# Gate one-hot blocks of a mixture kernel: stationary operand packed per token, moving operand with two tokens innermost

## The chip, the cores and the metric

The kernel runs on one core of a Trainium2 chip. The metric is the device time of one execution in microseconds (us), the median of the runs. The engines are named as the profile names them: PE is the matrix engine (PEld its weight loads, shown apart), DVE the vector engine, ACT the scalar engine, POOL GpSimd, SP the queue that issues most loads.

## The reference

Two models one after the other, two layers each, on 256 tokens of width 1024 (in the first model 256 context tokens run beside them in layer 0). The part that matters here is the feed-forward of the first model, in which 8 heads choose 16 of 16,384 experts for each token; each expert is addressed by two keys of 128:

```
s1, i1 = lax.top_k(s[:, :, 0], 16)
s2, i2 = lax.top_k(s[:, :, 1], 16)
cidx = i1[..., :, None] * 128 + i2[..., None, :]
top_s, pos = lax.top_k(s1[..., :, None] + s2[..., None, :], 16)
eidx = take_along_axis(cidx, pos)
gate = softmax(top_s)
hid = gelu(einsum('td,thkd->thk', x, u_emb[eidx]))
out = einsum('thk,thkd->td', gate * hid, v_emb[eidx])
```

So every token has 128 (head, choice) pairs, each with a first key, a second key and a gate.

## The kernel before

The kernel does not gather the chosen experts. It computes all 16,384 hidden values of every token (128 tiles of 128 experts, the loop over `i` in `peer`), and multiplies them by a gate matrix that is zero where an expert was not chosen. All large products are made from a high and a low part of both factors, three matmuls each (`mm3`, lines 408 to 410), on weights that the DVE, the ACT and at times POOL split into `wh` and `wl` (lines 179 and 190). Layer 0 has T = 512 tokens, so its matmuls have 512 columns; layer 1 has 256.

The gate matrix is made token by token. For one token, with the 128 (head, choice) pairs on the partitions, `Am` holds the one-hot of the second key (128 pairs by 128 keys) and `Bm` the one-hot of the first key times the gate; the product of the two over the pairs is the token's 128 by 128 gate matrix. The gate is kept in two float16 parts, so `Bm` has two halves (n = 0, 1), and a token takes two matmuls of 128 columns that add up in PSUM. `IT` holds the keys and `GT` the gates, in float16, pairs on partitions and tokens along the row.

The one-hots are made for eight tokens at a time (the loop over `q`, lines 1355 to 1369): the DVE compares a table `iota` with the keys (line 1359 for `Am`, line 1360 for `Bk`), and multiplies `Bk` by the two gate parts (line 1365, twice). All tiles have the shape [2, 128, 4]: four tokens lie innermost, so that in every operand the innermost run is four neighbouring float16. A token's operand on the PE is therefore a column of elements that are 8 bytes apart:

```
nc.tensor.matmul(b[:, j * 128:(j + 1) * 128], Am[:, :, j], Bm[:, n, :, j], ...)
```

`flush` (line 1335) takes four tokens: eight such matmuls (line 1343) into one PSUM bank, which the ACT then copies out (line 1344). There are 128 flushes in layer 0 and 64 in layer 1. A flush comes two loop steps after its tiles were made (`pend`); `Am` and `Bm` have three buffers, `Bk` two.

All of this is a side task. The main loop runs the expert tiles, and after every three main matmuls `tick` adds their estimated PE time to a clock; whenever the clock passes the next due time, the side task runs to its next `yield`. So the order of the instructions on each engine is fixed when the program is built, and the side task's place in it depends on estimates, not on measured times. While the gates are made, `W.pool_every` is 0 (line 1328), so all low parts `wl` of the streamed weights are made on the DVE, two tiles ahead of the PE. In layer 0 the DVE also makes modulation sums on the side (line 460).

Of the kernel before, what the change touches and what calls it, by code (L numbers as in the profile page):

```python
# [12 lines left out]
F16 = mybir.dt.float16  # L13
# [3 lines left out]
OP = mybir.AluOpType  # L17
# [330 lines left out]
def tile_dit_peer_conformer(ctx: ExitStack, tc: tile.TileContext, A, out):  # L348
    nc = tc.nc
# [6 lines left out]
    def bankA():  # L356
        return psum.tile([128, 512], F32, name="pA", bufs=4)
# [3 lines left out]
    def bankB():  # L361
        ring[0] += 1
        return psum.tile([128, 512], F32, name="pB", bufs=4)
# [228 lines left out]
    def tproj(key, X, T, bank=None, mid=None):  # L592
        h, lo = W.next(*key)
        p = bankA() if bank is None else bank
        for d in range(8):
            if mid is not None and d == 4:
                mid()
            mm3(p[:, :T], (h[:, d * 128:(d + 1) * 128], lo[:, d * 128:(d + 1) * 128]),
                (X[0][:, d, :T], X[1][:, d, :T]), d == 0, d == 7)
            tick(3 * T / 2.4)  # L600
        return p
# [595 lines left out]
    def peer(l, hcp, kp, keys, early):  # L1197
# [11 lines left out]
        with ExitStack() as st:  # L1209
            pp = st.enter_context(tc.tile_pool(name=f"peer{l}", bufs=1))  # L1210
            IT = pp.tile([128, 2, T], F16, name="IT")
            GT = pp.tile([128, 2, T], F16, name="GT")
            GN = pp.tile([128, nt, 128], F32, name="GN")
            IN = pp.tile([128, nt, 2, 128], F32, name="IN")
            iota = pp.tile([128, 128, 4], F16, name="iota")
            nc.gpsimd.iota(iota, pattern=[[1, 128], [0, 4]], base=0, channel_multiplier=0, allow_small_or_imprecise_dtypes=True)
            gp = st.enter_context(tc.tile_pool(name=f"gel{l}", bufs=3))
            if l == 0:
                ms_stack = ExitStack()
# [34 lines left out]
            def select():  # L1254
                yield from topk_keys()
                yield from route()
# [5 lines left out]
            for c in range(16):  # L1262
                p = early.pop(0)[0] if early else tproj(("wq", l, c), X, T)
                q = tk.tile([128, T], F32, name="q", bufs=4)
# [3 lines left out]
            def route():  # L1268
# [47 lines left out]
                for i in range(3):  # L1316
                    b = bankB()
# [13 lines left out]
                tg = tk_stack.enter_context(tc.tile_pool(name=f"gm{l}", bufs=1))  # L1331
                pend = []
                sg = None

                def flush(q, Am, Bm):
                    nonlocal sg
                    tb, r = divmod(q, TB // 4)
                    if r == 0:
                        sg = tg.tile([128, 128, TB], F32, name="gst", bufs=2)
                    b = bankB()  # L1340
                    for j in range(4):
                        for n in range(2):
                            nc.tensor.matmul(b[:, j * 128:(j + 1) * 128], Am[:, :, j], Bm[:, n, :, j], start=n == 0, stop=n == 1)  # L1343
                    nc.scalar.activation(sg[:, :, r * 4:r * 4 + 4].rearrange("p i t -> p t i"),  # L1344
                                         b.rearrange("p (t i) -> p t i", t=4), AF.Copy, scale=1.0 / GSCALE)
                    if r == TB // 4 - 1:
                        nc.scalar.dma_start(g_d[tb], sg)

                shape = [128, 2, 128, 4]
                iotas = iota[:, None].to_broadcast(shape)  # L1350

                def spread(x, q):
                    return x[:, q * 4:q * 4 + 8].rearrange("p (q t) -> p q t", t=4)[:, :, None, :].to_broadcast(shape)

                for q in range(0, T // 4, 2):
                    Am = tg.tile(shape, F16, name="Am", bufs=3)
                    Bk = tg.tile(shape, F16, name="Bk", bufs=2)
                    Bm = tg.tile([128, 2] + shape[1:], F16, name="Bm", bufs=3)
                    nc.vector.tensor_tensor(Am, iotas, spread(IT[:, 1], q), op=OP.is_equal)
                    nc.vector.tensor_tensor(Bk, iotas, spread(IT[:, 0], q), op=OP.is_equal)  # L1360
                    if len(pend) > 2:
                        flush(*pend.pop(0))
                    yield
                    for n in range(2):
                        nc.vector.tensor_mul(Bm[:, n], Bk, spread(GT[:, n], q))
                    if len(pend) > 2:
                        flush(*pend.pop(0))
                    pend.extend((q + j, Am[:, j], Bm[:, :, j]) for j in range(2))
                    yield
                for x in pend:  # L1370
                    flush(*x)
                    yield
# [31 lines left out]
            b = None  # L1404
            GB = 2 if not last else 4
            for i in range(128):
# [7 lines left out]
                if half == 0:  # L1414
                    b = bankA()
# [4 lines left out]
                if half == 512 // T - 1:  # L1420
                    n = 512 // T
                    j = i % GB - (n - 1)
# [25 lines left out]
            if not last:  # L1448
                for i in range(2):
                    t = hcp.tile([128, D], F32, name=f"hc{i}")  # L1450
# [552 lines left out]
    with tc.tile_pool(name="hcp", bufs=1) as hcp:  # L2003
        norm_ctx = peer(0, hcp, kp, *first)
        kp = ExitStack()
        first = mixer(1, kp, norm_ctx)
    peer(1, None, kp, *first)
    with tc.tile_pool(name="b2", bufs=1) as b2p:
        dec = b2p.tile([128, RET_H, 256], F32, name="dec")
# [154 lines left out]
```

## Time and profile before

| what | value |
|---|---|
| median of 3 runs | 4792.56 us (4787.25 to 4793.66) |
| the profiled execution's own time | 4791.03 us |
| its span, first to last instruction | 4789.2 us |
| mean granted PE clock, share of full speed | 0.984 |
| PE busy | 4624.7 us (97%) |
| DVE busy | 3018.0 us (63%) |
| the gate's 1536 matmuls of line 1343, busy | 213.9 us |
| the gate's 384 DVE operations, busy | 123.8 + 65.9 + 65.8 us |

The spans of one execution are compared with that execution's own time. Busy time of the PE says that some matmul was in flight: matmuls overlap, so what one costs is read from the distance between starts, not from its duration. The time that an engine waits matters only where the engine is the one that sets the pace.

### The profile page before, as it was taken

To read this page: it belongs to the slowest core of one execution; us is meant where nothing else is said; L and a number is where in the kernel's file an instruction comes from. 1 tells how busy PE (TensorE), PEld (TensorE's weight loads), DVE (VectorE), ACT (ScalarE), POOL (GpSimd) and SP (SyncE) were. 2 spreads that over 40 slices of the span, in tenths; PEclk is the share of its full clock that TensorE was granted. 3 is DMA by queue.
4 is the path that set the end of the run, shared out by engine and by line. 5 is a ranking of instruction groups with operands and counts; after the bars stand their busy time and mean duration, and the time that the engine had idled before them with its cause. 6 is when DMAs were issued, how large, how long until landed. Compare 5 with 4: busy or idle time off the path is not lost. (4 is left out here: it accounts for less than half of the span.)

```text
span 4789.2 us, 67997 instructions
## 1 busy us (share of the span) xinstructions
PE 4624.7 (97%) x26438; PEld 3984.8 (83%) x26438; DVE 3018.0 (63%) x4777; ACT 2047.0 (43%) x2979; POOL 1201.8 (25%) x884
## 2 busy tenths in 40 slices
PE   8999999999999999999999999999999988999799
PEld 5787878888888888888798889999888977999788
DVE  6847768798676333333466887765666586555865
ACT  4324443224554322222343454565444444444344
POOL 2412433330000422222213545102442043000510
PEclk9999999999999999999999999999999999999899
DMA  5422222455656655555453346668876533555344
GB/s 218 158 87 64 73 99 95 162 189 198 220 212 226 210 190 190 183 191 191 138 174 106 102 135 226 222 241 293 282 275 221 186 120 119 185 176 171 116 142 158
DMA packets 283357, 831.39 MB, mean 174 GB/s; under 512 B 23688, under 2 KB 106264, under 8 KB 273560
## 3 DMA queue, kind: packets, MB, share of 16 engines
q1 hardware_dynamic: 260960, 715.74, 45.2%
q10 hardware_dynamic: 21896, 110.24, 6.1%
q8 instruction: 207, 3.39, 0.3%
q14 instruction: 118, 0.97, 0.1%
q0 software_dynamic: 176, 1.06, 0.1%
HBM read 724.17 MB, written 102.77 MB: 173 GB/s over the span
## 5 line engine op out<-in xcount | busy, mean ns | idle before, releaser
L190 DVE TENSOR_TENSOR wl<-raw,wh 128x1024 fp32r<-128x1024 f32 (+1 forms) x893 | 1154.1, 1302 | 976.7 <-PE pB L1460 343.1
L179 ACT ACTIVATE wh<-raw 128x1024 fp32r<-128x1024 f32 (+1 forms) x1098 | 1144.1, 1045 | 1072.8 <-issue 709.4
L408 PE MATMUL pA<-xH,wh 128*128 128x256 f32 (+1 forms) x4696 | 1533.8, 327 | 3.6 <-ACT xH L413 1.3
L410 PE MATMUL pA<-xH,wl 128*128 128x256 f32 (+1 forms) x4696 | 1508.3, 321 | 14.1 <-DVE wl L190 12.4
L409 PE MATMUL pA<-xL,wh 128*128 128x256 f32 (+1 forms) x4696 | 1509.8, 322 | 0.5 <-DVE xL L414 0.3
L410 PEld LDWEIGHTS pA<-xH,wl 128*128 128x128 f32 x4696 | 893.3, 190 | 88.6 <-DVE wl L190 16.6
L408 PEld LDWEIGHTS pA<-xH,wh 128*128 128x128 f32 x4696 | 893.9, 190 | 77.9 <-issue 6.0
L409 PEld LDWEIGHTS pA<-xL,wh 128*128 128x128 f32 x4696 | 891.8, 190 | 68.2 <-DVE xL L414 1.1
L190 POOL TENSOR_TENSOR wl<-raw,wh 128x1024 fp32r<-128x1024 f32 (+2 forms) x205 | 479.6, 2342 | 901.2 <-PE pA L410 547.5
L1393 POOL TENSOR_TENSOR gelc<-gelc,gmc 128x512 f32<-128x512 f32 (+1 forms) x256 | 340.0, 1361 | 1004.3 <-DMA gmc<-gmat 699.7
L1460 PE MATMUL pA<-wl,Wh 128*128 128x512 f32 x1024 | 322.4, 395 | 0.0
L1460 PE MATMUL pA<-wh,Wh 128*128 128x512 f32 x1024 | 322.3, 395 | 0.0
L1460 PE MATMUL pA<-wh,Wl 128*128 128x512 f32 x1024 | 322.3, 395 | 0.0
L1344 ACT ACTIVATE gst<-pB 128x512 f32<-128x512 f32 x192 | 216.2, 1126 | 230.5 <-PE pB L1343 229.5
L408 PE MATMUL pA<-wh,xH 128*128 128x256 f32 (+2 forms) x800 | 287.1, 359 | 9.3 <-DVE cu L1833 7.7
L409 PE MATMUL pA<-wl,xH 128*128 128x256 f32 (+2 forms) x800 | 277.6, 347 | 6.5 <-POOL wl L190 5.9
L410 PE MATMUL pA<-wh,xL 128*128 128x256 f32 (+2 forms) x800 | 277.3, 347 | 1.2 <-DVE xL L414 1.1
L414 DVE TENSOR_TENSOR Wl<-gelc,Wh 128x512 fp32r<-128x512 f32 (+1 forms) x256 | 160.6, 628 | 171.3 <-ACT Wh L413 169.6
L1423 ACT ACTIVATE gstage<-pA 128x512 f32<-128x512 f32 x192 | 117.0, 609 | 292.8 <-PE pA L410 286.8
L399 POOL TENSOR_TENSOR segr<-segr,nhalf 128x1 f32<-128x1 f32 (+1 forms) x24 | 13.9, 578 | 907.9 <-DVE segr L490 907.9
L1460 PEld LDWEIGHTS pA<-wl,Wh 128*128 128x128 f32 x1024 | 191.9, 187 | 47.0
L1460 PEld LDWEIGHTS pA<-wh,Wl 128*128 128x128 f32 x1024 | 191.9, 187 | 47.0
(422 smaller groups left out, 6352.6 us busy)
## 6 DMA issues: line engine op xcount, KB each, us to landing
raw<-in_u SPq DMA_DIRECT2D x256, 512.0 KB, 3.8
raw<-in_vv SPq DMA_DIRECT2D x256, 512.0 KB, 3.8
gel<-gstage ACTq DMA_DIRECT2D x96, 512.0 KB, 3.7
gmat<-gst ACTq DMA_DIRECT2D x24, 2048.0 KB, 7.6
gelc<-gel SPq DMA_DIRECT2D x48, 1024.0 KB, 5.9
gmc<-gmat SPq DMA_DIRECT2D x48, 1024.0 KB, 9.5
raw<-in_modt SPq DMA_DIRECT2D x80, 512.0 KB, 3.7
raw<-in_conv SPq DMA_DIRECT2D x48, 512.0 KB, 3.6
```

The source lines that it names most:

```text
L179: self.nc.scalar.activation(h[:, :w], t[:, :w], AF.Copy)
L190: e.tensor_sub(lo[:, :w], t[:, :w], h[:, :w].bitcast(F32))
L399: nc.gpsimd.tensor_tensor(r, r, nhalf[:, 0:1].to_broadcast([128, w]), op=OP.pow)
L408: nc.tensor.matmul(o, s[0], m[0], start=start, stop=False)
L409: nc.tensor.matmul(o, s[0], m[1], start=False, stop=False)
L410: nc.tensor.matmul(o, s[1], m[0], start=False, stop=stop)
L414: nc.vector.tensor_sub(lo, src, h.bitcast(F32))
L1344: nc.scalar.activation(sg[:, :, r * 4:r * 4 + 4].rearrange("p i t -> p t i"), b.rearrange("p (t i) -> p t i", t=4), AF.Copy, scale=1.0 / G ...
L1393: nc.gpsimd.tensor_mul(gv, gv, m[:, :, ci])
L1423: nc.scalar.activation(gs[:, j:j + n].rearrange("p a t -> p (a t)"), b, AF.Gelu_apprx_tanh)
L1460: nc.tensor.matmul(acc[t][dh], s_, m_[:, dh * 512:(dh + 1) * 512], start=(i == 0 and n == 0), stop=(i == 127 and n == 2))
```

## The change

`Am` becomes [8, 128]: for each of the eight tokens its 128 elements lie side by side. It is made from a second table `iotac` that is read again for each token, and from the keys with each key repeated 128 times along the innermost dimension. `Bk` and `Bm` become [4, 128, 2] (per gate part): two tokens innermost in place of four, so a token's column of the moving operand has elements 4 bytes apart. The counts and sizes of the DVE operations and matmuls and their order on every engine stay as they are; POOL makes one more small table per layer.

```
-            iota = pp.tile([128, 128, 4], F16, name="iota")
-            nc.gpsimd.iota(iota, pattern=[[1, 128], [0, 4]], base=0, ...)
+            iota = pp.tile([128, 128, 2], F16, name="iota")
+            nc.gpsimd.iota(iota, pattern=[[1, 128], [0, 2]], base=0, ...)
+            iotac = pp.tile([128, 128], F16, name="iotac")
+            nc.gpsimd.iota(iotac, pattern=[[1, 128]], base=0, ...)
...
-                            nc.tensor.matmul(b[:, j * 128:(j + 1) * 128], Am[:, :, j], Bm[:, n, :, j], start=n == 0, stop=n == 1)
+                            nc.tensor.matmul(b[:, j * 128:(j + 1) * 128], Am[:, j], Bm[:, n, j // 2, :, j % 2], start=n == 0, stop=n == 1)
...
-                shape = [128, 2, 128, 4]
+                shape = [128, 4, 128, 2]
                 iotas = iota[:, None].to_broadcast(shape)
 
                 def spread(x, q):
-                    return x[:, q * 4:q * 4 + 8].rearrange("p (q t) -> p q t", t=4)[:, :, None, :].to_broadcast(shape)
+                    return x[:, q * 4:q * 4 + 8].rearrange("p (q t) -> p q t", t=2)[:, :, None, :].to_broadcast(shape)
 
                 for q in range(0, T // 4, 2):
-                    Am = tg.tile(shape, F16, name="Am", bufs=3)
+                    Am = tg.tile([128, 8, 128], F16, name="Am", bufs=3)
                     Bk = tg.tile(shape, F16, name="Bk", bufs=2)
                     Bm = tg.tile([128, 2] + shape[1:], F16, name="Bm", bufs=3)
-                    nc.vector.tensor_tensor(Am, iotas, spread(IT[:, 1], q), op=OP.is_equal)
+                    nc.vector.tensor_tensor(Am, iotac[:, None, :].to_broadcast([128, 8, 128]),
+                                            IT[:, 1, q * 4:q * 4 + 8, None].to_broadcast([128, 8, 128]), op=OP.is_equal)
                     nc.vector.tensor_tensor(Bk, iotas, spread(IT[:, 0], q), op=OP.is_equal)
...
-                    pend.extend((q + j, Am[:, j], Bm[:, :, j]) for j in range(2))
+                    pend.extend((q + j, Am[:, 4 * j:4 * j + 4], Bm[:, :, 2 * j:2 * j + 2]) for j in range(2))
```

## Rows read from the trace of the kernel before

**Rows 1.** The page: busy time of the engines (share of the span), and 40 slices.

```profile
PE 4624.7 (97%) x26438; PEld 3984.8 (83%) x26438; DVE 3018.0 (63%) x4777; ACT 2047.0 (43%) x2979; POOL 1201.8 (25%) x884
...
PE   8999999999999999999999999999999988999799
```

**Rows 2.** Busy time by stretch, two in layer 0's gate stage, one in layer 1's.

```profile
core 0: us, PE busy (x) PEld busy (x) DVE busy (x) ACT busy (x) POOL busy (x), PEclk, DMA share, GB/s
1120.00:1200.00 80.00, 80.00 (x443) 64.32 (x442) 62.21 (x94) 42.12 (x44) 0.00 (x0) 1.00 0.60 208
1200.00:1480.00 280.00, 280.00 (x1536) 225.09 (x1534) 193.42 (x283) 149.45 (x157) 0.00 (x0) 1.00 0.60 215
3040.00:3240.00 200.00, 200.00 (x1675) 196.71 (x1674) 132.69 (x168) 125.63 (x134) 0.00 (x0) 1.00 0.67 234
```

**Rows 3.** PE in order of time, layer 0: start, us, line, out<-in, shape.

```profile
1123.91 1.11 PE L1343 MATMUL pB<-Bm,Am 128*128 128x128 f16 x8
1124.78 0.48 PE L408 MATMUL pA<-xH,wh 128*128 128x512 f32 x1
1125.09 0.39 PE L409 MATMUL pA<-xL,wh 128*128 128x512 f32 x1
1125.32 0.39 PE L410 MATMUL pA<-xH,wl 128*128 128x512 f32 x1
...
1127.42 0.40 PE L410 MATMUL pA<-xH,wl 128*128 128x512 f32 x1
1127.66 1.11 PE L1343 MATMUL pB<-Bm,Am 128*128 128x128 f16 x8
```

**Rows 4.** PE in order of time, layer 1.

```profile
3059.86 0.28 PE L410 MATMUL pA<-xH,wl 128*128 128x256 f32 x1
3059.98 1.11 PE L1343 MATMUL pB<-Bm,Am 128*128 128x128 f16 x8
3060.84 0.37 PE L408 MATMUL pA<-xH,wh 128*128 128x256 f32 x1
3061.05 0.28 PE L409 MATMUL pA<-xL,wh 128*128 128x256 f32 x1
3061.17 0.28 PE L410 MATMUL pA<-xH,wl 128*128 128x256 f32 x1
```

**Rows 5.** Groups by shape, PE and PEld, whole span: busy us, mean ns.

```profile
L408 PE MATMUL pA<-xH,wh 128*128 128x256 f32 x3136 | 901.1, 287 | 3.6 <-ACT xH L413 1.3 <-ACT tmpa L684 0.8 <-ACT wh L179 0.8
L1343 PE MATMUL pB<-Bm,Am 128*128 128x128 f16 x1536 | 213.9, 296 | 0.0
...
L408 PEld LDWEIGHTS pA<-xH,wh 128*128 128x128 f32 x4696 | 893.9, 190 | 77.9 <-issue 6.0 <-ACT xH L413 1.9 <-DVE xL L559 1.1
...
L1343 PEld LDWEIGHTS <-Am 128*128 128x128 f16 x1536 | 156.3, 119 | 40.0 <-issue 32.9 <-DVE Am L1359 0.8 <-DVE sjunk L460 0.5
```

**Rows 6.** Groups by shape on the DVE, 1120 to 1480 us.

```profile
L1365 DVE TENSOR_TENSOR Bm<-Bk,GT 128x1024 f16<-128x1024 f16 x112 | 72.3, 687 | 1.1
L190 DVE TENSOR_TENSOR wl<-raw,wh 128x1024 fp32r<-128x1024 f32 x47 | 57.6, 1225 | 84.2 <-issue 51.4 <-ACT gst L1344 27.7 <-PE pA L410 4.3
L1359 DVE TENSOR_TENSOR Am<-iota,IT 128x1024 f16<-128x1024 f16 x55 | 37.8, 687 | 18.1 <-PE pB L1343 18.0
L1360 DVE TENSOR_TENSOR Bk<-iota,IT 128x1024 f16<-128x1024 f16 x55 | 37.7, 686 | 0.0
```

**Rows 7.** Line 1298, a comparison in f32 with a repeated innermost element: ns min/median/max.

```profile
L1298 DVE TENSOR_TENSOR eq<-abf,iota x24: 1210/1220/3316, 877.5 to 3014.0; 128x1024 f32<-128x1024 f32 x24
```

**Rows 8.** Waits of PEld in layer 0's gate stage, 1116 to 1520 us.

```profile
PEld L1343 <- issue: 31.6, 115, 0.3
PEld L1343 <- DVE Am L1359: 0.8, 3, 0.3
PEld L1343 <- DVE sjunk L460: 0.5, 2, 0.3
PEld L1343 <- DVE Bm L1365: 0.5, 2, 0.3
PEld L1343 <- DVE wl L190: 0.3, 1, 0.3
```

**Rows 9.** The table's making on POOL, once per layer.

```profile
L1216 POOL IOTA iota<- x2: 1195/1198/1201, 719.6 to 2807.3; 128x512 f16 x2
```

More of the change, by code (lines that the diff above doesn't have):

```diff
@@ L1214, in peer @@
             IN = pp.tile([128, nt, 2, 128], F32, name="IN")
-            iota = pp.tile([128, 128, 4], F16, name="iota")
-            nc.gpsimd.iota(iota, pattern=[[1, 128], [0, 4]], base=0, channel_multiplier=0, allow_small_or_imprecise_dtypes=True)
+            iota = pp.tile([128, 128, 2], F16, name="iota")
+            nc.gpsimd.iota(iota, pattern=[[1, 128], [0, 2]], base=0, channel_multiplier=0, allow_small_or_imprecise_dtypes=True)
+            iotac = pp.tile([128, 128], F16, name="iotac")
+            nc.gpsimd.iota(iotac, pattern=[[1, 128]], base=0, channel_multiplier=0, allow_small_or_imprecise_dtypes=True)
             gp = st.enter_context(tc.tile_pool(name=f"gel{l}", bufs=3))
```

## The prediction

> **What bounds the kernel now.** The page's first two parts come first: the PE is busy for 97% of the span and in nearly every slice for nine tenths or more, the DVE for 63% [rows 1]. Then the two stages in which the gate is made, as stretches: in all three the PE is busy for the whole stretch, at a granted clock of 1.00 (the 2.4 GHz level), while the DVE is busy for 78%, 69% and 66% of them and POOL for nothing [rows 2]. So here the PE sets the pace, and DVE time costs nothing until it makes the PE wait. The list of waits shows the same: PEld waited for the DVE for 2.1 us in 8 waits over the whole of layer 0's stage [rows 8]; the 31.6 us against "issue" stand beside a PE that is still streaming, so they are no loss.
>
> Next, what a flush costs on the PE. In layer 0 two flushes start 3.75 us apart, at 1123.91 and 1127.66 [rows 3]. Twelve main matmuls lie between them. Their step is 0.233 us: ten steps from 1125.09 to 1127.42. That is 2.80 us, and 0.95 us is left for the eight float16 matmuls. Layer 1 agrees: with a step of 0.12, the first matmul behind the flush would be at 3060.93 by its successor's start at 3061.05, 0.95 us after 3059.98 [rows 4]. There are 192 flushes (1536 matmuls, eight each [rows 5]), so the gate's matmuls take 182 us of PE time that nothing hides.
>
> Within a flush: eight matmuls last 1.11 us from the first start to the last end, and one lasts 0.296 [rows 3, 5]; the seven steps between starts are (1.11 - 0.296) / 7 = 0.116 us each. Is that much for 128 columns? The f32 matmuls answer: 512 columns step in 0.233 and 256 in 0.12 us [rows 3, 4], hence (0.233 - 0.120) / 256 = 0.44 ns a column and 7 ns fixed, and 128 columns would step in 0.063 us. The float16 matmuls need nearly twice that. Their duration says it too: 296 ns for 128 columns against 287 for 256 columns of f32 [rows 5]. What differs is the layout: f32 columns lie 4 bytes apart, these 8 bytes.
>
> **The change part by part.**
>
> *The PE.* The moving operand's columns move from 8 to 4 bytes apart, the distance at which the f32 columns stream at 0.44 ns; the stationary operand becomes dense. I take the step of 0.063 us, worked out above. Counting seven steps (what stands behind the eighth is an f32 weight load, which does not change), a flush saves 7 x (0.116 - 0.063) = 0.37 us, and 192 flushes save 71 us. Bounds: nothing, if the step does not come from the layout, and 8 steps, 81 us. I exclude a loss here, as both operands only come closer together. I take 0.063 because the rows of f32 show 4 bytes at that rate on the same engine and because the matmul's own duration is long, not just its distance.
>
> Against it stands a rule of the Trainium skill (page "SBUF — State Buffer", section "Door 1: The DMA port swizzle"): reads keep their full bandwidth as long as at least two of them fall into one 16-byte line, which 2-byte elements at 8 bytes still do. By it the moving operand would already stream at full rate and this term would be nothing. The step of 0.116 against 0.063 speaks against it, but no row tells the moving operand's share from the weight load's; this is rival C.
>
> *The DVE, Am.* Its 96 operations (8 tokens each) now last 0.687 us [rows 6]. One operand will have an innermost element that is repeated 128 times, and no float16 row shows that. Bounds: 0.687 (the pace kept), and what 1024 elements take at one at a time, 1.22 us, in f32 for line 190 and for the comparison of line 1298, which also repeats its innermost element [rows 6, 7]. I take 1.22, as line 1298 is the same operation with the same kind of operand: 0.53 x 96 = 51 us more DVE time. What hides it: from 1120 to 1480 us the DVE is busy for 62.2 + 193.4 = 255.6 of 360 us [rows 2], which leaves 104 idle. The 55 Am operations there [rows 6] add 29, the PE's gain shortens the stretch by 360 / 3.4 x 0.37 = 39 (a flush every 3.4 us on average, between 3.05 and 3.75), and 36 us are still idle. In layer 1: 67 idle of 200, less 15 and less 21, leaves 31. Tight is only layer 0's beginning: 17.8 idle of 80, less 12 x 0.53 = 6.4 and less 8.7, leaves under 3. There the queue is nearly full, and what is queued behind an Am are Bk, Bm and the low parts wl, for which the PE waits two tiles later. I charge the 6 us that the longer Am adds in these 80 us as stall. Bounds: 0 and all 51.
>
> *The DVE, Bk and Bm.* 96 and 192 operations of 0.687 us [rows 6] keep a run of neighbouring float16 in every operand, two long where it was four. I leave their cost alone; bounds: 0, and 288 x 0.53 = 153 us of DVE time (rival D).
>
> *POOL.* One table of 128x512 took 1.20 us per layer [rows 9]; now there are two, a half and a quarter of it in size. Bounds: 1.2 us less or more per layer, far ahead of the gate stage. Nothing. Waits, buffers and DMAs are the same in number and order.
>
> *What is late next.* With the PE's period for two flushes down from 6.8 to 6.06 us, the DVE is the next engine, at 89% of layer 0's stage (255.6 + 29 over 360 - 39). ACT stays far below (42 of 80 us, 53% [rows 2]).
>
> *Sum.* 4791.0 (the profiled execution) - 71 + 6 = 4726. The median of the runs lies 1.5 us above that execution, so 4727.5; I say 4728.
>
> **The rivals.** A is the sum above, with its own range from 4710 (8 steps, no stall) to 4750 (half of the Am time unhidden).
>
> B: half a gain. A weight load lasts 119 ns on average [rows 5], about the step itself, so the load may be a second limit behind the moving stream, and the step ends halfway, near 0.090: 7 x 0.026 x 192 = 35 us saved, 4763 with the stall. For it: load and step are equally long today. Against it: f32 loads of 190 ns [rows 5] hide under steps of 0.12 [rows 4].
>
> C: the step stays. The load of the next weights starts with a matmul and takes what it takes, however they lie; the longer Am is hidden, as 75 us of the DVE's 104 stay idle without the PE's gain. 4791 + 2 = 4793, and 4794 against the median. For it: the equality of load and step again. By the Trainium skill (page "TensorE: Matmul & The Clock Gate", section "LDWEIGHTS (loading the stationary operand)") the time of a load goes by its number of columns, 107 ns for 128; an estimate by it is a step of 0.107, some 12 us saved and 4785. No row here shows a float16 load that nothing else slows.
>
> D: slower. A run of two tokens is too short for the DVE's fast pace, and Bk and Bm fall to 1.22 us like Am. Then from 1120 to 1480 the DVE needs 255.6 + 29 + (55 + 112) x 0.53 = 373 us [rows 2, 6], more than the PE's 360; it becomes the bound, whatever the PE gains, and layer 0's 400 us get some 15 us longer. Layer 1 (132.7 + 15 + 46 = 194 of 200 us) just hides it. 4791 + 15 + 1.5 = 4808. It decides from the point at which two flushes ask for more than 6.8 us of DVE time; today it is 4.8. Against it: at four tokens the operation takes 0.687 us for 1024 elements, so short runs as such cost nothing there. The Trainium skill (page "Vector Engine (DVE) Microarchitecture Reference", section "5.1 Performance modes — why throughput varies by op and dtype") also counts two neighbouring elements as enough for the fast pace.
>
> **How the numbers follow.** A 0.54, B 0.13, C 0.22, D 0.09, and 0.02 for what I don't see. About 0.2%, 9.6 us, is what a measurement can tell from no change. Faster by more: A, nearly all of B, and a little of C: 0.68. Within: most of C: 0.15. Slower: D, and C with a stall of over 8 us: 0.17. The range goes from 4712 to 4804: it takes in A but for its last end, B and C with a stall of up to 10 us, and leaves out D.
>
> **What would show it.** Right: line 1343's eight matmuls span about 0.70 us instead of 1.11 and one lasts well under 287 ns; flushes in layer 0 start 2.68 or 3.38 us apart; line 1359 lasts 1.22 us, lines 1360 and 1365 stay at 0.69; PEld's waits for the DVE stay under 10 us. Wrong: the flush keeps its 0.95 us (C), lines 1360 and 1365 go to 1.22 (D), or the stretches show a PE that idles while the DVE is full: then the gain was there and the DVE gave it back.

## The result and the profile after

The changed kernel takes 4708.17 us (median of 4 runs, 4706.73 to 4712.31) against 4793.11 before: a ratio of 0.9827, 95% interval 0.981 to 0.9844, or 85 us less. The profiled execution took 4707.19 us with a span of 4705.4, 83.8 shorter than before. The forecast was 4728, in a range from 4712 to 4804: the direction and the mechanism came out as said, but more was gained than the range allowed, because two terms of the sum were mis-sized. In the new kernel the lines behind the tables stand two or three later: 1345 is the gate's matmul, 1361 `Am`, 1363 `Bk`, 1368 `Bm`.

The PE in order of time, layer 0, after (start, us, line, out<-in, shape), which answers to [rows 3]:

```profile
1121.83 0.63 PE L1345 MATMUL pB<-Bm,Am 128*128 128x128 f16 x8
1122.27 0.48 PE L408 MATMUL pA<-xH,wh 128*128 128x512 f32 x1
1122.59 0.40 PE L409 MATMUL pA<-xL,wh 128*128 128x512 f32 x1
...
1124.93 0.40 PE L410 MATMUL pA<-xH,wl 128*128 128x512 f32 x1
1125.16 0.63 PE L1345 MATMUL pB<-Bm,Am 128*128 128x128 f16 x8
```

The flushes start 3.33 us apart with twelve main matmuls between them: 3.33 - 12 x 0.233 = 0.53 us for a flush in place of 0.95. All instances of the line, after (min/median/max ns):

```profile
L1345 PEld LDWEIGHTS <-Am x1536: 95/96/101, 1119.2 to 3179.7; 128*128 128x128 f16 x192
L1345 PE MATMUL pB<-Bm,Am x1536: 218/218/233, 1119.2 to 3179.7; 128*128 128x128 f16 x192
```

A matmul lasts 218 ns, 78 less than in [rows 5]; the step is (0.63 - 0.218) / 7 = 0.059 us. The DVE from 1120 to 1440 us, after, against [rows 6] (which goes to 1480):

```profile
L1368 DVE TENSOR_TENSOR Bm<-Bk,GT 128x1024 f16<-128x1024 f16 x114 | 73.6, 687 | 1.2
L1361 DVE TENSOR_TENSOR Am<-iotac,IT 128x1024 f16<-128x1024 f16 x57 | 69.5, 1220 | 3.9 <-PE pB L1345 3.9
L1363 DVE TENSOR_TENSOR Bk<-iota,IT 128x1024 f16<-128x1024 f16 x57 | 39.1, 685 | 0.0
```

`Am` went from 687 to 1220 ns; the operations with a run of two kept their 0.69 us. The stretches, after, against [rows 2]:

```profile
core 0: us, PE busy (x) PEld busy (x) DVE busy (x) ACT busy (x) POOL busy (x), PEclk, DMA share, GB/s
1120.00:1200.00 80.00, 80.00 (x505) 62.02 (x504) 76.70 (x103) 48.79 (x52) 0.00 (x0) 1.00 0.66 240
1200.00:1440.00 240.00, 240.00 (x1510) 186.10 (x1509) 212.27 (x279) 144.36 (x154) 0.00 (x0) 1.00 0.69 248
```

The DVE is busy for 96% and 88% of them, and the PE still never idles. PEld's waits for the DVE from 1116 to 1480 us, after, sum to 9.9 us in 36 waits, of 0.3 at most; the two largest groups:

```profile
PEld L1345 <- DVE Am L1361: 3.6, 13, 0.3
PEld L1345 <- DVE Bk L1363: 3.3, 12, 0.3
```

They cost the PE nothing that the stretches show, where it is busy throughout.

Where the time went is read from one marker that stands ahead of the gate stage in each layer, the key matmuls. Before, line 1239 (first to last start, layer 0, then layer 1):

```profile
L1239 PE MATMUL pB<-keys,q x128: 272/275/275, 732.6 to 828.2; 128*128 128x128 f32 x128
...
L1239 PE MATMUL pB<-keys,q x64: 271/275/377, 2821.0 to 2869.4; 128*128 128x128 f32 x64
```

and after, line 1241:

```profile
L1241 PE MATMUL pB<-keys,q x128: 272/275/275, 730.9 to 826.5; 128*128 128x128 f32 x128
...
L1241 PE MATMUL pB<-keys,q x64: 270/275/377, 2764.7 to 2813.2; 128*128 128x128 f32 x64
```

From the last key matmul of layer 0 to the first of layer 1 it took 2821.0 - 828.2 = 1992.8 us, now 1938.2: 54.6 less, for 128 flushes. From the last of layer 1 to the end of the span: 4789.2 - 2869.4 = 1919.8, now 1892.2: 27.6 less, for 64 flushes. That is 0.427 and 0.431 us a flush, so both layers agree with the 0.42 read from two flushes (0.95 - 0.53), and 192 x 0.42 = 81 of these 82 us. What is left, 1.7 us, lies ahead of the gate stage, where the kernels differ in nothing but the small tables on POOL; the first marker of the ten profiled kernels of this document lies anywhere from 730.9 to 739.4 us, so 1.7 us says nothing.

### The profile page after: what moved, and what is told of

It reads as the page before. It is cut to its first block, busy times and chain, and to the rows that moved or that the text cites. A ratio compares the mean times of both kernels' runs of the same rounds, so it can differ in the third digit from the quotient of the medians.

```text
span 4705.4 us, 68002 instructions
## 1 busy us (share of the span) xinstructions
PE 4540.7 (96%) x26438; PEld 3901.7 (83%) x26438; DVE 3066.3 (65%) x4777; ACT 2045.9 (43%) x2979; POOL 1199.3 (25%) x886
```

## The experiments

The prediction could not say which operand's layout held the step at 0.116 us. Theory M: the moving stream. Theory W: the load of the weights. Theory S: both, on one limit. The first three kernels and the one with both operands at 16 bytes ran beside the kernel before at a median of 4790.2 us (7 runs, 4787.6 to 4796.2), the other four beside it at 4791.6 (9 runs, 4787.1 to 4797.0). Six of the eight kernels ran once, so a few us between single times mean little; there the two distances between the markers, which leave out what happens ahead of the gate stage, are the better measure. In most edits below only the telling lines are shown; tables, tile shapes and slices follow them.

**One operand alone, and both at 4 bytes.** The stationary operand dense, the moving one as before:

```
-nc.tensor.matmul(..., Am[:, :, j], Bm[:, n, :, j], ...)
+nc.tensor.matmul(..., Am[:, j], Bm[:, n, :, j], ...)
```

> Only the stationary operand is dense (as in the change, with its slower Am operation); the moving one keeps its elements 8 bytes apart. Theory M (the moving stream at 8 bytes apart sets the step): the step of the gate's matmuls stays at 0.116 us, a matmul still lasts near 296 ns, a flush costs 0.95 us, and the time is 4793, within 5 us. Theory W (the load of the spread weights sets the step): the step falls to 0.058 us, a flush costs 0.53 us, and the time is about 4708. Theory S (both share one limit on reads): a step in between, near 0.087, and about 4750.

The moving operand with two tokens innermost, the stationary one as before:

```
+nc.tensor.matmul(..., Am[:, :, j], Bm[:, n, j // 2, :, j % 2], ...)
```

> Only the moving operand has its elements 4 bytes apart (as in the change); the stationary one keeps 8 bytes, and its Am operation keeps 0.687 us. Theory M: the step falls to 0.058 us, a flush costs 0.53 us, the time is about 4708, and the DVE is 51 us less busy than in the change. Theory W: the step stays at 0.116 us and the time is 4793, within 5 us. Theory S: near 0.087 and 4750.

Both with two tokens innermost, so that no DVE operation gets slower:

```
+nc.tensor.matmul(..., Am[:, j // 2, :, j % 2], Bm[:, n, j // 2, :, j % 2], ...)
```

> Two tokens innermost in both operands, so both are read 4 bytes apart, and all four DVE operations keep 0.687 us. Theory M: the step is 0.058 us as in the change; DVE busy time falls by 51 us against it (3066 to 3015), which changes nothing, as the change showed no wait for it: 4708, within 5 us of the change. Theory W: weights at 4 bytes load faster than at 8, but slower than dense ones: a step between 0.058 and 0.116, 4710 to 4790. If the longer Am cost the change time after all, this one is faster than it by up to 6 us, the stall that was charged.

Measured: 4789.84 and 4716.35 us (one run each) and 4709.78 us (median of 4, 4701.52 to 4713.14; ratio 0.9829, 0.9813 to 0.9846). All instances of the gate's matmul, of the dense stationary operand alone:

```profile
L1345 PEld LDWEIGHTS <-Am x1536: 95/115/118, 1123.6 to 3260.8; 128*128 128x128 f16 x192
L1345 PE MATMUL pB<-Bm,Am x1536: 274/294/296, 1123.6 to 3261.0; 128*128 128x128 f16 x192
```

of the moving operand alone:

```profile
L1345 PEld LDWEIGHTS <-Am x1536: 111/113/137, 1122.4 to 3187.4; 128*128 128x128 f16 x192
L1345 PE MATMUL pB<-Bm,Am x1536: 217/221/253, 1122.4 to 3187.4; 128*128 128x128 f16 x192
```

and of both at 4 bytes:

```profile
L1343 PEld LDWEIGHTS <-Am x1536: 96/97/103, 1121.5 to 3181.7; 128*128 128x128 f16 x192
L1343 PE MATMUL pB<-Bm,Am x1536: 217/218/233, 1121.5 to 3181.7; 128*128 128x128 f16 x192
```

M holds. A dense stationary operand leaves the matmul at 294 ns and the time where it was; the moving operand brings it to 221 ns and nearly all the gain. In the first of the three the load's fastest instance takes 95 ns, the median 115: beside a slow moving stream even a dense load reads as long as the step. That is what had made the load look like a second limit. With the moving operand alone at 4 bytes, the two distances between the markers (829.7 to 2770.8 us, and 2819.2 to the end at 4714.6) are together 6.1 us longer than in the change. They come from the stationary operand: with loads of 113 ns instead of 97, the second of the eight matmuls starts 0.09 us behind the first (in the flush at 1199.87 us) in place of 0.06 (the change's at 1121.83), and the other steps hardly grow.

The third kernel's markers, at a span of 4707.3 us:

```profile
L1239 PE MATMUL pB<-keys,q x128: 272/275/275, 733.2 to 828.8; 128*128 128x128 f32 x128
...
L1239 PE MATMUL pB<-keys,q x64: 271/275/377, 2766.7 to 2815.2; 128*128 128x128 f32 x64
```

Its distances, 1937.9 and 1892.1 us, are those of the change (1938.2 and 1892.2) within 0.4 us, although its `Am` operations take 51 us less. So the longer `Am` costs the change nothing that can be measured, and a dense stationary operand brings nothing over one at 4 bytes. The times alone could not have told this from a stall of 6 us.

**Farther apart.** Eight tokens innermost in both operands, 16 bytes from element to element:

```
-shape = [128, 2, 128, 4]
+shape = [128, 1, 128, 8]
```

> Eight tokens innermost in both operands: elements 16 bytes apart, DVE operations 0.687 us as before. If the cost grows with the distance (each element its own access), the step doubles again from 0.116 to about 0.23 us, a flush costs 0.95 + 8 x 0.115 = 1.87 us and the time is 4793 + 192 x 0.92 = 4970. If 8 bytes apart already pays all there is to pay, the step stays at 0.116 us and the time at 4793, within 5 us.

And eight innermost in the stationary operand alone, the moving one at 4 bytes (the edit is against the change):

```
+shape8 = [128, 1, 128, 8]
...
-Am = tg.tile([128, 8, 128], F16, name="Am", bufs=3)
+Am = tg.tile(shape8, F16, name="Am", bufs=3)
```

> Moving operand 4 bytes apart as in the change, stationary operand 16 bytes apart. Theory M with a load that hides: the step stays at 0.058 to 0.062 us, only the load at the end or start of a flush gets longer: 4708 to 4722. If the load has a limit of its own that 8 bytes just stayed under, the step goes to that limit: at 0.116, which is what a stream 8 bytes apart needs, 4793.

Measured: 4977.76 and 4729.60 us, one run each. The PE in order of time with both at 16 bytes:

```profile
1195.40 2.06 PE L1343 MATMUL pB<-Bm,Am 128*128 128x128 f16 x8
1197.10 0.60 PE L408 MATMUL pA<-xH,wh 128*128 128x512 f32 x1
...
1200.10 2.06 PE L1343 MATMUL pB<-Bm,Am 128*128 128x128 f16 x8
```

Twelve main matmuls lie between, so a flush costs 4.70 - 2.80 = 1.90 us; a matmul lasts 413 ns, and the step is (2.06 - 0.413) / 7 = 0.235 us. It doubled again, as expected if the cost goes with the distance; both operands moved here, and the next kernel shows that the stationary one's share is small. With the stationary operand alone at 16 bytes:

```profile
L1345 PEld LDWEIGHTS <-Am x1536: 141/146/173, 1122.3 to 3200.8; 128*128 128x128 f16 x192
L1345 PE MATMUL pB<-Bm,Am x1536: 219/226/287, 1122.3 to 3200.8; 128*128 128x128 f16 x192
```

and two of its flushes in order of time:

```profile
1195.92 0.71 PE L1345 MATMUL pB<-Bm,Am 128*128 128x128 f16 x8
1196.44 0.48 PE L408 MATMUL pA<-xH,wh 128*128 128x512 f32 x1
...
1198.64 0.73 PE L1345 MATMUL pB<-Bm,Am 128*128 128x128 f16 x8
```

The load grows to 146 ns, yet the matmul stays at 226 and the flush at 0.62 us (2.72 us between flushes with nine main matmuls): the load hides but for 0.09 us a flush, 17 us in all. Most of that is at the flush's start: in the second flush shown the second matmul starts 0.13 us behind the first, and the other steps are near 0.063. The time is 8 us above the 4708 to 4722 that M gave, and far from 4793.

**The DVE.** `Am` alone made slow, in the layout of before, by writing it token by token into the spread tile:

```
-nc.vector.tensor_tensor(Am, iotas, spread(IT[:, 1], q), op=OP.is_equal)
+nc.vector.tensor_tensor(Am.rearrange("p q k t -> p q t k"), iotac[:, None, None, :].to_broadcast([128, 2, 4, 128]),
+                        IT[:, 1, q * 4:q * 4 + 8].rearrange("p (q t) -> p q t", t=4)[:, :, :, None].to_broadcast([128, 2, 4, 128]), op=OP.is_equal)
```

> Layouts and matmuls as before the change, but the Am operation walks key by key within a token and so takes 1.22 us or more in place of 0.687: the change's DVE cost alone. If that cost is hidden under a PE that sets the pace (as the change and the dense stationary operand alone showed), the step stays at 0.116 us and the time at 4791, within 5 us. If the charge of the prediction holds, it is 6 us slower, 4797.

Measured: 4791.20 us (one run). It took 2.5 us an operation, twice what was meant, which makes the test harder:

```profile
L1361 DVE TENSOR_TENSOR Am<-iotac,IT 128x1024 f16<-128x1024 f16 x96 | 239.8, 2498 | 2.0 <-PE pB L1345 1.8
```

174 us more in `Am` operations than before, the DVE busy for 79.48 us of the 80 behind 1120 us and the PE for all 80, and the time did not move. The PE has its old, longer flushes here; that the charge of 6 us falls in the change too is shown by the kernel with both operands at 4 bytes, above. Then both operands dense, with `Am`, `Bk` and `Bm` all at 1.22 us, which is rival D's load:

```
-shape = [128, 2, 128, 4]
+shape = [128, 8, 128]
```

> Both operands dense per token (2 bytes apart); Am, Bk and both Bm operations repeat their innermost element and take 1.22 us each: rival D's load on the DVE together with the PE's gain. Theory M: dense is no faster than 4 bytes apart, the step is 0.057 us. If a full DVE sets the pace (rival D's sum: 373 us of DVE work per 360 us of the stage before in layer 0, 194 per 200 in layer 1), layer 0's stage is some 15 us longer than before and layer 1's some 6 us shorter, 4800, and PEld's waits for the DVE, 12 us in the change, grow to over 50. If DVE work is never the bound here, the time is 4708.

Measured: 4784.23 us (one run, span 4782.2). The stretches of layer 0, the PE's longest wait over the whole span, a flush that did not wait, and the markers:

```profile
core 0: us, PE busy (x) PEld busy (x) DVE busy (x) ACT busy (x) POOL busy (x), PEclk, DMA share, GB/s
1120.00:1200.00 80.00, 71.31 (x427) 54.44 (x426) 79.52 (x81) 39.85 (x44) 0.00 (x0) 0.98 0.54 185
1200.00:1520.00 320.00, 287.37 (x1729) 218.38 (x1729) 318.24 (x323) 159.58 (x175) 0.00 (x0) 0.97 0.59 214
```

```profile
PE pB L1343 <- DVE Bm L1365: 45.5, 53, 2.0
```

```profile
1201.21 0.62 PE L1343 MATMUL pB<-Bm,Am 128*128 128x128 f16 x8
```

```profile
L1239 PE MATMUL pB<-keys,q x128: 272/275/275, 736.3 to 831.5; 128*128 128x128 f32 x128
...
L1239 PE MATMUL pB<-keys,q x64: 271/275/377, 2829.4 to 2877.9; 128*128 128x128 f32 x64
```

Here the DVE is the bound: busy for over 99%, and the PE idles for a tenth of layer 0's stage. Nearly all of the gain is given back, though the time stays 7 us below that of before instead of 9 above. The markers part the two layers: between them 1997.9 us, 5.1 more than before (15 were expected), and behind them 1904.3, 15.5 less than before (6 were expected). So layer 0 lost its whole gain of 54.6 us and some more, and layer 1 kept over half of its 27.6. The 45.5 us of waiting for `Bm` all lie in layer 0's stage. They are not all that layer 0 lost against the change (59.7 us); the granted clock, 0.98 and 0.97 in the two stretches, may have a share in the rest, which no run separates. PEld waited for `Bm` for 33.5 us there, where over 50 had been expected. Dense moving columns are no faster than those at 4 bytes beyond what can be read: matmuls last 219 ns at the median, and the step is (0.62 - 0.219) / 7 = 0.057 us. So rival D was a real way to lose the gain; the run of two is what kept the change away from it.

**Sixteen in a row.** Both at 4 bytes, with two flushes back to back:

```
-                    if len(pend) > 2:
-                        flush(*pend.pop(0))
                     yield
...
                     if len(pend) > 2:
                         flush(*pend.pop(0))
+                        flush(*pend.pop(0))
```

> Two tokens innermost in both operands, and two flushes always back to back: sixteen gate matmuls in a row. In the change a flush costs 0.53 us, of which 8 x 0.058 = 0.46 are the matmuls and the rest the switch to the f32 weights. If the switch is paid once for sixteen, 96 x 0.06 = 6 us are saved against the change: 4702. If the bunched flushes make the PE wait for the ACT's copies or the DVE, it is no faster than the change, 4708 or above.

Measured: 4706.22 us (5 runs, 4701.11 to 4709.67; ratio 0.9821, 0.9808 to 0.9835). The intervals of this kernel and of the change overlap, so the times do not settle it. The marker does, for the profiled executions:

```profile
L1239 PE MATMUL pB<-keys,q x128: 272/275/275, 739.4 to 835.0; 128*128 128x128 f32 x128
...
L1239 PE MATMUL pB<-keys,q x64: 270/275/377, 2769.4 to 2817.9; 128*128 128x128 f32 x64
```

Between the layers it takes 2769.4 - 835.0 = 1934.4 us, 3.8 less than the change, and from there to the end of its span of 4706.7 it takes 1888.8, 3.4 less. Against the kernel with the same layouts and flushes of eight it is 3.5 and 3.3 less, so the 7 us come from the bunching and not from the shorter `Am`. That agrees with the 6 expected from paying the switch to f32 weights once for sixteen matmuls; what in the switch costs them was not looked into. This execution reached its first marker 8.5 us later than the change did, in a part where the kernels differ only in POOL's tables, and that hid it in the total.

## Why the prediction was right, and where it was wrong

- **The bound.** Right. The PE is full in both gate stages before and after, and a shorter flush shortens the kernel by as much: 81 us by flushes, 82 by the markers.
- **The step and its cause.** Right in kind. Said 0.063 us, measured 0.059 after; said to come from the moving stream at 8 bytes, and M held in all the kernels that moved the operands' distances, with a small share for the stationary operand (6 us at 8 bytes, about 17 at 16).
- **The PE's term, 7 x (0.116 - 0.063) = 0.37 us a flush and 71 us in all.** This is the first step that failed: a flush gained 0.42 us, so the term should have been 81. About half of the lack is the step: seven steps gained 7 x 0.057 = 0.40. The rest is the count of seven. Of what stands behind the eighth matmul the prediction says that it "does not change", but the first main matmul came 0.02 us sooner as well, probably because the eighth's own stream is shorter too. That the bound of eight steps, 81 us, hits the measured 81 is luck in part, as it takes eight of the smaller steps; eight times the measured 0.057 would be 88.
- **The 6 us charged "as stall".** This is the second step that failed; the stall was nothing. The room was worked out well: under 3 us of idle DVE in the first 80 us, and 80 - 76.70 = 3.3 were measured. But a DVE that is nearly full was taken for one that makes the PE wait. The PE is busy throughout that stretch, and the kernel in which `Am` keeps 0.69 us takes as long from marker to marker, within 0.4 us. Even with `Am` at 2.5 us and 0.5 us of idle DVE, under the old flushes, nothing was lost. That the tiles are made two steps ahead may be what evens it out; no run changed that.
- **What the two make together.** 16 of the 20 us by which the forecast was too slow; another 1.7 lies ahead of the gate stage, and the last 2 are rounding of the 0.42 and of where the median lies beside the profiled execution.
- **The range.** Its lower end, 4712, is where the sum lands with the better bound of both terms (4791.0 - 81 + 1.5). A's own range went to 4710, and the prediction left this last end out; the measured 4708 lies below both.
- **`Am` at 1.22, `Bk` and `Bm` at 0.69 us.** Right, 1.220 and 0.685 to 0.687. The Trainium skill's rule (page "Vector Engine (DVE) Microarchitecture Reference", section "5.1 Performance modes — why throughput varies by op and dtype") that two neighbouring elements are enough agrees with it.
- **Rival B.** Fell: the load's equality with the step was the step's own doing. A load of 113 ns beside a moving operand at 4 bytes cost 6 us, not half the gain.
- **Rival C.** Fell, and with it the rules named beside it. The Trainium skill (page "SBUF — State Buffer", section "Door 1: The DMA port swizzle") lets 2-byte elements at 8 bytes stream freely; here they took 0.116 us for 128 columns against 0.059 at 4 bytes, so the measurement decides against it for the PE's moving operand. The Trainium skill's 107 ns for a weight load of 128 columns (page "TensorE: Matmul & The Clock Gate", section "LDWEIGHTS (loading the stationary operand)") cannot be a limit where loads follow each other every 0.059 us. The 4785 us set beside C keeps A's 6 us of stall; with C's own 2 us it is 4791 + 2 - 12 = 4781.
- **Rival D.** Did not come about, as the run of two kept its pace; dense `Bk` and `Bm` showed its mechanism, with 4784 in place of the 4800 expected of that kernel. Both layers came out some 10 us better than the sums of the DVE's work said; why was not tried.

## What to carry to other kernels

Read what a matmul costs from the distance between starts and compare it, per column, with another matmul of the same kernel: a step that is too long for its columns can come from the moving operand's layout, and changing one operand at a time tells. Lay out a 2-byte moving operand so that its columns are at most 4 bytes apart; in this kernel runs of two keep the DVE's pace of 0.69 us for 1024 elements, where a fully dense layout needs a repeated element and 1.22. DVE time that grew under a full PE cost nothing here until the DVE itself was full, so a thin reserve is not yet a stall. When single times scatter by more than the effect, compare the time between two markers instead.

## What the runs showed of the hardware that was not expected

The step of a 128-column float16 matmul at a granted clock of 1.00 goes with the distance of the moving columns from 4 bytes up: 0.059 us at 4 bytes, 0.116 at 8, 0.235 at 16, and hardly other for dense columns (219 ns a matmul against 218, in stretches at 0.97 and 0.98). Why the engine needs this was not looked into. The stationary operand's distance works on the load (97, 113 and 146 ns at 4, 8 and 16 bytes, beside a moving operand at 4), and most of that hides under the stream: a flush gets 0.03 and 0.09 us longer, mostly at its first step. A comparison that writes float16 elements 8 bytes apart took 2.5 us where the same one writing densely took 1.22.
